# One core, hybrid decoder trunk: weight additions also given out during rotations, and another order of the last tokens' chain

## The chip, the core and the metric

The kernel runs on one core of a Trainium2 chip. A core has a matrix engine (TensorE, PE in the profile), whose weight loads are shown apart (PEld), and VectorE (DVE), ScalarE (ACT), GpSimd (POOL) and SyncE (SP). Each engine works through its own row of instructions in order and waits on semaphores for what others make. DMAs are given out by an engine (here nearly all by SP, some by POOL and ACT) and run beside it. The metric is the device time of one execution in microseconds (us); lower is better.

## The reference

The computation is one decoder layer in fp32 on 512 tokens of width 1024: a norm, an input projection, two token mixers (causal pooling, and a sparse attention with compressed, selected and window branches), a merge by sigmoid gates, `w_out`, a second norm, and an MLP of width 4096 with a squared ReLU, and a last norm. Cut to what matters here:

```python
def reference(x, norm_mix, w_in, ..., w_out, norm_mlp, w_ff1, w_ff2, norm_final):
    for l in range(DEPTH):
        h = rms_norm(x, norm_mix[l])
        proj = h @ w_in[l]
        u, q, kc, vc, ksl, vsl, kwn, vwn, g_nsa, g_merge = jnp.split(proj, IN_SPLITS, axis=-1)
        y_pool = pool_mixer(u, w_pool[l], pool_scale[l])
        y_nsa = nsa_mixer(q, kc, vc, ksl, vsl, kwn, vwn, g_nsa, ...)
        g_a, g_b = jnp.split(jax.nn.sigmoid(g_merge), 2, axis=-1)
        merged = g_a * (y_pool @ w_proj_pool[l]) + g_b * (y_nsa @ w_proj_nsa[l])
        x = x + merged @ w_out[l]
        h = rms_norm(x, norm_mlp[l])
        x = x + jnp.square(jax.nn.relu(h @ w_ff1[l])) @ w_ff2[l]
    return rms_norm(x, norm_final)
```

In the attention each of 16 heads has scores of queries against keys, a softmax under a causal mask, and a product with the values. The sequence is 512 long and the window 512, so that the work per head is a triangle of blocks of 128 x 128 to 128 x 512.

## The kernel before

**Number format.** A product in fp32 is made of three products of a faster type: each operand is split into a high part (ACT, names ending in H or h, L395 and L521) and a low part (DVE, names ending in L or l, L401 and L524), and high x high, low x high and high x low are summed in PSUM.

**Fewer products.** The large matrix products (the gates, `w_out`, `w_ff1`, `w_ff2`) are done by Strassen's scheme in Winograd's form: of four quarters of each operand seven products are made instead of eight. Their names stand in the code as `A11`, `A12`, `A22`, `S1` to `S4`. For these, sums of quarters of the weights are needed. The kernel forms these sums in HBM, ahead of their use: `make_sum` (L333 to L342) gives out a copy on SP (L340, tiles named S) behind a load of raw weights, and `add_sum` (L344 to L348) gives out a DMA on POOL (L348) that adds another quarter to what the copy has written. A list `jobs` holds the sums in a fixed order, `begun` those whose copy is given out and whose addition is not; the additions are taken from its front. Some sums are sums of earlier ones: job 93 copies job 91's sum (S_110_93 <- S_110_91) and adds to it. The finished sums are loaded on SP (L299) like other weights.

**The attention** takes from 172 to 365 us. It runs as 96 slots, eight pairs of heads by 12 slots. A slot has scores on PE (L1378), a masked maximum on DVE (L1400), exponentials on ACT (L1410), reciprocals on DVE (L1420), the weights on POOL (L1423: the P of a slot, times the reciprocal and the gate; one or two instructions of 128 x 128 to 128 x 512), and four slots later (LAG) the transposes of P on PE (L1440), their copies by ACT and DVE (L1451, L1456), and products with the values (L1474). Between these PE does products of the projections as filler (L565). Beside the slots run side steps: the rotation of the next head pair's queries (a DMA on SP, multiplications on POOL at L899) and the compressed branch's gates (POOL L1331 to L1335). `scored["rope"]` is true while a rotation is under way. In the slot loop an addition is given out behind the weights of the slot before, in every third slot in which no rotation is under way and more than two sums are begun:

```python
            if i > 7 and i % 3 == 0 and not scored["rope"] and len(begun) > 2:
                add_sum(last)
```

**The junction** lies between 430 and 460 us, where `w_out` ends and `w_ff1` begins. Class `Mixed` ends `w_out`: its last product S4 (L565) is added to x by `end` (L1821 to L1825) for the tokens 2 and 3 (a token here is a row block of 128 tokens), the others by `take` (L1827 to L1848). Then `scaled` norms a block into a tile xs (DVE L1612) and `to_fm` turns it (PE L1864, against `ident`), copies and splits it (ACT L1868, DVE L1871), and forms the sums T1 to T3 of the blocks (L1878, L1883). The first products of `w_ff1` are made by class `Group` (PE L635; its banks are emptied by ACT L650 and DVE L656 to L670): four key names in the order A11100, A11101, A12100, A12101, then the S1 ones, which need T1. The order in which PE takes the transposes and products comes from a scheduler that goes by readiness and priority in program order; `behind(x)` (L783) keeps an instruction behind x. After the junction the rest of `w_ff1` and `w_ff2` (class `Wide`, PE L1685, its results added to x at L1706) run without a break to 741 us, then the last norm.

Of the kernel before, what the change touches and what calls it, by code (L numbers as in the profile page):

```python
# [16 lines left out]
ALU = mybir.AluOpType  # L17
# [45 lines left out]
def trunk(ctx: ExitStack, tc: tile.TileContext, A, out):  # L63
# [548 lines left out]
    def until(ready):  # L612
        while not ready():
            assert side
            step_side()

    class Group:


# [6 lines left out]
        def pe(self, o):  # L626
            until(lambda: o not in self.NEEDS or self.NEEDS[o] in self.done)
            if not self.done:
                side.append(self.main())
            name, x, *at = self.X[o]  # L630
            until(lambda: self.of(x))
            moving = self.of(x)

            def mm(out, w, f, k, u, v, **kw):
                PE.matmul(out, w[u][:, k, 128 * f:128 * f + 128], moving[v][:, k, :], **kw)  # L635
            if not at:
                self.ps[name] = self.bank()
            product(self.ps[name], o + self.key, not at, mm)
            if at:
                side.append(self.last(name, *at))  # L640
            self.done.add(o)
# [30 lines left out]

    hT = (R1, R2)
    f_banks = [2]
    last_mm = [None]

    def fm_products(wH, wL, xT, sub=0, nk=8, tok=slice(0, S)):
        prods = []
# [104 lines left out]
    def behind(made):  # L783
        return tc.issue_after(made.ins)
# [463 lines left out]
    with ExitStack() as c2:  # L1248
# [249 lines left out]
        for i in range(n + LAG + PLAG):  # L1498
# [18 lines left out]
            if 0 <= i - 1 < n:  # L1517
                last = weight(i - 1)
                slot.update(long=i > 3 and slots[i - 1][1] == 1, scaled=last)
            if i > 7 and i % 3 == 0 and not scored["rope"] and len(begun) > 2:  # L1520
                add_sum(last)
            if 0 <= t < n:
                slot["low"] = turn_lo(t)
# [196 lines left out]
    with ExitStack() as c3:  # L1720
# [80 lines left out]
        class Mixed(Wide):  # L1801
# [18 lines left out]
            def end(self, f, ps):  # L1820
                yield  # L1821
                x = XX[:, 2 + f, 0:512]
                DVE.tensor_tensor(x, x, ps, op=ALU.add)
                square_sum(2 + f, 0, 1)
                yield from to_fm(2 + f)  # L1825

            def take(self, o, ps):  # L1827
                yield from super().take(o, ps)
# [12 lines left out]
                elif o == "A22":  # L1841
                    for t in range(2):
                        square_sum(t, 1)
                    xs = [scaled(t) for t in range(2)]
                    while "S1" not in self.done:
                        yield
                    for t in range(2):
                        yield from to_fm(t, xs[t])  # L1848

        def scaled(t):  # L1850
            xs = q3.tile([128, D], F32, tag="xs", bufs=2, name="xs")
# [3 lines left out]
        def to_fm(t, xs=None):  # L1855
# [5 lines left out]
            for a in range(2):  # L1861
                pt = bank()
                for k in range(4):
                    PE.transpose(pt[:, 128 * k:128 * k + 128], xs[:, 512 * a + 128 * k:512 * a + 128 * k + 128], ident)  # L1864
                src = pt[:, :].rearrange("p (k c) -> p k c", k=4)
                b = f"{a + 1}{th + 1}"
                if b != "12":
# [252 lines left out]
```

## Time and profile before

| | us |
|---|---|
| median of 3 runs | 768.44 (767.5 to 770.75) |
| the profiled execution | 766.66 |
| its span | 764.9 |
| attention | 172 to 365 |
| junction of w_out and w_ff1 | 430 to 452 |
| w_ff1 and w_ff2 | 452 to 741 |

The span is the time from the first to the last instruction in the trace; the profiled execution's time has a little around it. Its mean granted clock was 0.997 of full speed. PE is busy most of the span, so the page is read from the rows in which PE waits, and from the work around them; an idle DVE, ACT or POOL counts only where PE waits for what it makes.

### The profile page before, as it was taken

What the parts mean: (1) busy time and instruction counts of PE and PEld (TensorE: products, weight loads), DVE (VectorE), ACT (ScalarE), POOL (GpSimd) and SP (SyncE); (2) the same over time, 40 slices, a digit from 0 to 9 for tenths busy, and PEclk for the clock granted to TensorE, in tenths of its full rate; (3) what the DMA queues carried; (4) which work ended last, traced back from release to release, by engine and by line L of the source; (5) the groups of instructions that cost most, each with busy time, mean ns of one, the idle gap of its engine ahead of it and who ended that gap; (6) DMA issues with size and microseconds to landing.
All of it is one profiled execution on the core that took longest, in us unless ns stands there. A gap on an engine that the chain in (4) does not pass through costs nothing.

```text
span 764.9 us, 13254 instructions
## 1 busy us (share of the span) xinstructions
PE 752.9 (98%) x4661; PEld 669.7 (88%) x4661; DVE 670.8 (88%) x1282; ACT 513.2 (67%) x977; POOL 190.5 (25%) x269
## 2 busy tenths in 40 slices
PE   8999999999999999999999999999999999999996
PEld 7889999888888888888888799989998999899985
DVE  7998989549989889989689999998899788978897
ACT  7777655328878888898746576944774477447754
POOL 5001010117747876875000020111111111110001
PEclk9999999999999999999999999999999999999998
DMA  9869886986063945675383699979999999798532
GB/s 303 227 177 275 230 245 143 250 215 165 18 204 83 224 94 115 121 139 111 89 296 133 218 272 249 298 210 325 290 269 211 315 307 263 206 313 252 195 109 110
DMA packets 120285, 158.09 MB, mean 207 GB/s; under 512 B 6006, under 2 KB 88474, under 8 KB 119963
## 3 DMA queue, kind: packets, MB, share of 16 engines
q1 hardware_dynamic: 98058, 127.62, 51.2%
q0 software_dynamic: 21872, 28.84, 24.4%
q10 hardware_dynamic: 288, 0.79, 0.3%
q8 instruction: 37, 0.61, 0.3%
q14 instruction: 30, 0.24, 0.1%
HBM read 152.50 MB, written 59.77 MB: 278 GB/s over the span
## 4 chain that ended last, share of the span: by engine, by line
PE 87%; DVE 6%; ACT 2%; DMA 2%; issue 1%; POOL 1%; ACTq 0%; DVEq 0%; POOLq 0%; SPq 0%
PE psB L1685 21%; PE psB L635 21%; PE psF L565 18%; PE psV L635 5%; PE psB L565 4%; PE psS L1378 4%; PE psO L1474 3%; PE psT L1440 3%; PE psV L565 2%; PE psF L697 2%; DMA S<-w_ff 1%; PE psC L997 1%; DVE P L1400 1%; DVE PT L1456 1%; PE psT L565 1%
## 5 line engine op out<-in xcount | busy, mean ns | idle before, releaser
L348 POOL DMA_DIRECT2D S<-w_ff x44 | 49.3, 1124 | 334.1 <-DMA S<-w_ff 247.9
L395 ACT ACTIVATE wh<-raw 128x1024 fp32r<-128x1024 f32 x72 | 76.1, 1058 | 75.6 <-PE psB L635 28.3
L565 PE MATMUL psF<-R,wh 128*128 128x512 f32 x384 | 124.5, 400 | 0.0
L1423 POOL TENSOR_SCALAR P<-P,sm,GT 128x128 f32<-128x128 f32 (+3 forms) x128 | 91.0, 798 | 45.5 <-DVE sm L1420 25.4
L401 DVE TENSOR_TENSOR wl<-raw,wh 128x1024 fp32r<-128x1024 f32 x72 | 87.9, 1221 | 10.2 <-ACT wh L395 9.7
L565 PEld LDWEIGHTS psF<-R,wh 128*128 128x128 f32 x384 | 68.8, 188 | 11.2
L1410 ACT ACTIVATE P<-P,sm 128x128 f32<-128x128 f32 (+3 forms) x128 | 71.0, 557 | 9.6 <-DVE sm L1400 6.3
L565 PE MATMUL psF<-R,wl 128*128 128x512 f32 x192 | 75.5, 393 | 0.0
L521 ACT ACTIVATE wh<-raw 128x512 fp32r<-128x512 f32 (+1 forms) x76 | 45.1, 616 | 31.0 <-PE psF L565 21.2
L1400 DVE CUSTOM_DVE_ANT_0 P<-psS,cst 128x128 f32<-128x128 f32 (+3 forms) x128 | 59.5, 483 | 5.2 <-PE psT L1440 3.7
L395 ACT ACTIVATE w3h<-raw 128x1024 fp32r<-128x1024 f32 x36 | 38.1, 1058 | 36.9 <-PE psB L635 15.4
L524 DVE TENSOR_TENSOR wl<-raw,wh 128x512 fp32r<-128x512 f32 (+1 forms) x74 | 50.9, 697 | 11.0 <-ACT wh L521 10.2
L1451 ACT ACTIVATE PT<-psT 128x512 fp32r<-128x512 f32 (+2 forms) x96 | 49.0, 520 | 13.8 <-PE psT L1440 12.8
L1456 DVE TENSOR_TENSOR PT<-psT,PT 128x512 fp32r<-128x512 f32 (+2 forms) x96 | 56.2, 592 | 1.2 <-ACT PT L1451 1.0
L1440 PE MATMUL psT<-ident,P 128*128 128x128 f32 x320 | 50.2, 273 | 0.3 <-POOL P L1423 0.3
L401 DVE TENSOR_TENSOR w3l<-raw,w3h 128x1024 fp32r<-128x1024 f32 x36 | 44.0, 1222 | 5.6 <-ACT w3h L395 5.4
L1474 PE MATMUL psO<-PT,VV 128*128 128x256 f32 x320 | 48.5, 286 | 0.0
L635 PE MATMUL psB<-R,wh 128*128 128x256 f32 x336 | 46.7, 279 | 0.7 <-ACT GB L650 0.7
L1440 PEld LDWEIGHTS psT<-ident,P 128*128 128x128 f32 x320 | 39.5, 140 | 8.8 <-POOL P L1423 0.8
L635 PEld LDWEIGHTS psB<-R,wh 128*128 128x128 f32 x336 | 42.6, 188 | 1.1 <-ACT GB L650 0.9
L1474 PEld LDWEIGHTS psO<-PT,VV 128*128 128x128 f32 x320 | 42.2, 188 | 1.3 <-ACT PT L1451 0.3
L565 PEld LDWEIGHTS psF<-R,wl 128*128 128x128 f32 x192 | 36.0, 188 | 7.5
(450 smaller groups left out, 2074.6 us busy)
## 6 DMA issues: line engine op xcount, KB each, us to landing
raw<-w_ff SPq DMA_DIRECT2D x54, 512.0 KB, 6.0
S<-w_ff POOLq DMA_DIRECT2D x44, 512.0 KB, 8.5
raw<-S SPq DMA_DIRECT2D x44, 512.0 KB, 5.6
S<-w_ff SPq DMA_DIRECT2D x32, 512.0 KB, 7.6
raw<-w_in SPq DMA_DIRECT2D x31, 512.0 KB, 5.4
S<-S SPq DMA_DIRECT2D x12, 512.0 KB, 5.8
S_o<-w_out POOLq DMA_DIRECT2D x8, 512.0 KB, 7.8
raw<-w_proj_nsa SPq DMA_DIRECT2D x8, 512.0 KB, 4.5
```

The source lines that it names most:

```text
L395: ACT.activation(h, t, AF.Copy)
L401: DVE.tensor_tensor(l, t, h.bitcast(F32), op=ALU.subtract)
L524: eng.tensor_tensor(l[:, sl], t[:, sl], h[:, sl].bitcast(F32), op=ALU.subtract)
L565: PE.matmul(ps, a, b, start=first and j == 0, stop=last and j == n - 1, skip_group_check=True)
L635: PE.matmul(out, w[u][:, k, 128 * f:128 * f + 128], moving[v][:, k, :], **kw)
L1400: DVE.tensor_tensor_reduce(out=P[:, o:o + n].rearrange("p (a c) -> p a c", c=128), in0=s, in1=m, scale=1.0, scalar=3e38, op0=ALU.add, op1= ...
L1410: last_exp[:] = [ACT.activation(c, c, AF.Exp, bias=sm[:, 0, e:e + 1], scale=-1.0, accum_out=sm[:, 1, e:e + 1])]
L1423: r = POOL.tensor_scalar(P[:, o:o + n], P[:, o:o + n], sm[:, 2, e:e + 1], GT[:, qb, c + e:c + e + 1], op0=ALU.mult, op1=ALU.mult)
L1440: PE.transpose(pt[:, 128 * j:128 * j + 128], P[:, 128 * j:128 * j + 128], ident)
L1456: return DVE.tensor_tensor(dL, src, dH.bitcast(F32), op=ALU.subtract)
L1474: PE.matmul(ps[:, qb % 2, :, :], VV[:, k, b, g, :], t[:, j, :, :], start=False, stop=last and j == len(kbs) - 1 and t is tL, skip_group_ch ...
L1685: PE.matmul(ps[f], self.Y.of(y)[u][:, 2 * g + k, 128 * f:128 * f + 128], w[v][:, k, :], start=first and g == k == u == v == 0, stop=g == k ...
```

## The change

The sums are the same, and so are the instructions; what changes is when additions are given out, and the order at the junction. Four edits:

1. In the slot loop an addition is given out also while a rotation is under way, then in every sixth slot instead of every third.
2. In `Mixed.end` the addition of S4 to x, the sum of squares and `scaled` have a higher priority (60), and `to_fm` begins only after 30 (block 2) or 42 (block 3) products of the A11 group's keys with "10" have been given out (`fed`).
3. In `Mixed.take` only block 0 is normed ahead of S1; block 1 is normed behind the first addition of S1 to x.
4. The transposes of blocks 2 and 3 stand behind the last A11 product given out so far (`last_mm`), and the first A12100 product behind the last A11 product. `last_mm` is now made ahead of class `Group`.

```diff
--- before.py
+++ after.py
@@ -614,6 +614,8 @@
             assert side
             step_side()
 
+    last_mm, fed = [None], [0]
+
     class Group:
 
 
@@ -632,7 +634,12 @@
             moving = self.of(x)
 
             def mm(out, w, f, k, u, v, **kw):
-                PE.matmul(out, w[u][:, k, 128 * f:128 * f + 128], moving[v][:, k, :], **kw)
+                late = o + self.key == "A12100" and f == k == u == v == 0
+                with behind(last_mm[0]) if late else nullcontext():
+                    r = PE.matmul(out, w[u][:, k, 128 * f:128 * f + 128], moving[v][:, k, :], **kw)
+                if o == "A11":
+                    last_mm[0] = r
+                    fed[0] += self.key[:2] == "10"
             if not at:
                 self.ps[name] = self.bank()
             product(self.ps[name], o + self.key, not at, mm)
@@ -672,7 +679,6 @@
 
     hT = (R1, R2)
     f_banks = [2]
-    last_mm = [None]
 
     def fm_products(wH, wL, xT, sub=0, nk=8, tok=slice(0, S)):
         prods = []
@@ -1517,7 +1523,7 @@
             if 0 <= i - 1 < n:
                 last = weight(i - 1)
                 slot.update(long=i > 3 and slots[i - 1][1] == 1, scaled=last)
-            if i > 7 and i % 3 == 0 and not scored["rope"] and len(begun) > 2:
+            if i > 7 and i % (6 if scored["rope"] else 3) == 0 and len(begun) > 2:
                 add_sum(last)
             if 0 <= t < n:
                 slot["low"] = turn_lo(t)
@@ -1820,9 +1826,13 @@
             def end(self, f, ps):
                 yield
                 x = XX[:, 2 + f, 0:512]
-                DVE.tensor_tensor(x, x, ps, op=ALU.add)
-                square_sum(2 + f, 0, 1)
-                yield from to_fm(2 + f)
+                with tc.high_priority(60):
+                    DVE.tensor_tensor(x, x, ps, op=ALU.add)
+                    square_sum(2 + f, 0, 1)
+                    xs = scaled(2 + f)
+                while fed[0] < (30, 42)[f]:
+                    yield
+                yield from to_fm(2 + f, xs)
 
             def take(self, o, ps):
                 yield from super().take(o, ps)
@@ -1841,11 +1851,13 @@
                 elif o == "A22":
                     for t in range(2):
                         square_sum(t, 1)
-                    xs = [scaled(t) for t in range(2)]
+                    xs = scaled(0)
                     while "S1" not in self.done:
                         yield
-                    for t in range(2):
-                        yield from to_fm(t, xs[t])
+                    with behind(summed[0]):
+                        other = scaled(1)
+                    yield from to_fm(0, xs)
+                    yield from to_fm(1, other)
 
         def scaled(t):
             xs = q3.tile([128, D], F32, tag="xs", bufs=2, name="xs")
@@ -1861,7 +1873,8 @@
             for a in range(2):
                 pt = bank()
                 for k in range(4):
-                    PE.transpose(pt[:, 128 * k:128 * k + 128], xs[:, 512 * a + 128 * k:512 * a + 128 * k + 128], ident)
+                    with behind(last_mm[0]) if th else nullcontext():
+                        PE.transpose(pt[:, 128 * k:128 * k + 128], xs[:, 512 * a + 128 * k:512 * a + 128 * k + 128], ident)
                 src = pt[:, :].rearrange("p (k c) -> p k c", k=4)
                 b = f"{a + 1}{th + 1}"
                 if b != "12":
```

What this does to the rows of the engines is shown at four places, before and after. Lines below the first edit are 4, 6 or 13 higher in the changed kernel (L1423 is L1429, L899 is L905, L635 is L639, L1706 is L1712, L1864 is L1877, L1823 is L1830); L348 and L401 are the same.

POOL, at the head pair that is under way at 302 us; first before. P is the slot's weights, S a weight sum, rx and rs the rotation, cw and PC the compressed branch.

```order
L1423 TENSOR_SCALAR P<-P,sm,GT 128x384
L348 DMA S_111_95<-w_ff 512x1x256
L1423 TENSOR_SCALAR P<-P,sm,GT 128x384
L899 TENSOR_TENSOR rx<-rx,cst 128x256
L1331 TENSOR_TENSOR c_3794<-c_3794,GT 128x8
L1332 TENSOR_TENSOR cw<-cw,c_3794 128x8x32
L1423 TENSOR_SCALAR P<-P,sm,GT 128x512
L899 TENSOR_TENSOR rs<-rs,cst 128x256
L1334 TENSOR_SCALAR PC<-cw 128x4x64
L1335 TENSOR_TENSOR PC<-cw,PC 128x4x64
L1423 TENSOR_SCALAR P<-P,sm,GT 128x512
```

Then the changed kernel.

```order
L1429 TENSOR_SCALAR P<-P,sm,GT 128x384
L348 DMA S_111_95<-w_ff 512x1x256
L1429 TENSOR_SCALAR P<-P,sm,GT 128x384
L348 DMA S_100_83<-w_ff 512x1x256
L905 TENSOR_TENSOR rx<-rx,cst 128x256
L1429 TENSOR_SCALAR P<-P,sm,GT 128x512
L905 TENSOR_TENSOR rs<-rs,cst 128x256
L1337 TENSOR_TENSOR c_3797<-c_3797,GT 128x8
L1338 TENSOR_TENSOR cw<-cw,c_3797 128x8x32
L1340 TENSOR_SCALAR PC<-cw 128x4x64
L1341 TENSOR_TENSOR PC<-cw,PC 128x4x64
L1429 TENSOR_SCALAR P<-P,sm,GT 128x512
```

A second addition (S_100_83) now stands one weight behind the first, ahead of the rotation, and the compressed branch's steps have moved behind a 128x512 weight.

POOL at the last head pair, from 331.6 us in the trace of before.

```order
L1423 TENSOR_SCALAR P<-P,sm,GT 128x384
L348 DMA S_200_88<-w_ff 256x1x512
L1423 TENSOR_SCALAR P<-P,sm,GT 128x384
L1423 TENSOR_SCALAR P<-P,sm,GT 128x512 x2
L348 DMA S_100_83<-w_ff 512x1x256
L1423 TENSOR_SCALAR P<-P,sm,GT 128x128 x4
L1423 TENSOR_SCALAR P<-P,sm,GT 128x256 x2
L348 DMA S_201_89<-w_ff 256x1x512
```

The same place in the changed kernel.

```order
L1429 TENSOR_SCALAR P<-P,sm,GT 128x384
L348 DMA S_110_91<-w_ff 512x1x256
L1429 TENSOR_SCALAR P<-P,sm,GT 128x384
L1429 TENSOR_SCALAR P<-P,sm,GT 128x512 x2
L348 DMA S_110_92<-w_ff 512x1x256
L1429 TENSOR_SCALAR P<-P,sm,GT 128x128 x2
L348 DMA S_110_93<-w_ff 512x1x256
L1429 TENSOR_SCALAR P<-P,sm,GT 128x128 x2
L1429 TENSOR_SCALAR P<-P,sm,GT 128x256 x4
```

The additions here are now those of the sums 91, 92 and 93, and the last one stands between the first and the second two of the four 128x128 weights; before, those four stood together and an addition came behind the next two.

DVE at the junction, from the first normed blocks on (xs), before.

```order
L1612 SCALAR_TENSOR_TENSOR xs<-x_4903,sq,gB_4914 128x512 x2
L1602 RECIPROCAL sq<-sq 128x1
L1612 SCALAR_TENSOR_TENSOR xs<-x_4903,sq,gB_4914 128x512 x2
L1706 TENSOR_TENSOR x_4903<-x_4903,psB 128x512 x2
L401 TENSOR_TENSOR W1L<-raw_5221,W1H 128x1024
L1595 TENSOR_SCALAR sq<-sq 128x1
L401 TENSOR_TENSOR wl_5170<-raw_5239,wh_5169 128x1024
L1595 TENSOR_SCALAR sq<-sq 128x1
L1871 TENSOR_TENSOR R_65<-psB,R_64 128x4x128 x2
L401 TENSOR_TENSOR w3l<-raw_5257,w3h 128x1024
L1871 TENSOR_TENSOR R_65<-psB,R_64 128x4x128 x2
L1823 TENSOR_TENSOR x_4903<-x_4903,psB 128x512 x2
```

And in the changed kernel.

```order
L1618 SCALAR_TENSOR_TENSOR xs<-x_4903,sq,gB_4914 128x512 x2
L1712 TENSOR_TENSOR x_4903<-x_4903,psB 128x512 x2
L1608 RECIPROCAL sq<-sq 128x1
L401 TENSOR_TENSOR W1L<-raw_5221,W1H 128x1024
L1601 TENSOR_SCALAR sq<-sq 128x1
L1618 SCALAR_TENSOR_TENSOR xs<-x_4903,sq,gB_4914 128x512
L1601 TENSOR_SCALAR sq<-sq 128x1
L1618 SCALAR_TENSOR_TENSOR xs<-x_4903,sq,gB_4914 128x512
L1884 TENSOR_TENSOR R_65<-psB,R_64 128x4x128
L1830 TENSOR_TENSOR x_4903<-x_4903,psB 128x512
L1884 TENSOR_TENSOR R_65<-psB,R_64 128x4x128 x2
L401 TENSOR_TENSOR wl_5170<-raw_5239,wh_5169 128x1024
```

The two additions of S1 to x (L1706, now L1712) stand ahead of the second pair of xs, and S4's addition to the first of the later blocks (L1823, now L1830) ahead of two of the splits.

PE at the junction, around the first A12100 products (R_64 or R_65 against wh_5169) and the later blocks' transposes (ident,xs), before.

```order
L635 MATMUL psB<-R_64,W1L 128x256 x4
L635 MATMUL psB<-R_64,wh_5169 128x256
L635 MATMUL psB<-R_65,wh_5169 128x256
L1864 MATMUL psB<-ident,xs 128x128 x4
L635 MATMUL psB<-R_64,wh_5169 128x256
L635 MATMUL psB<-R_65,wh_5169 128x256
L1864 MATMUL psB<-ident,xs 128x128 x4
L635 MATMUL psB<-R_64,W1H 128x256
```

And in the changed kernel.

```order
L639 MATMUL psB<-R_65,W1H 128x256
L1877 MATMUL psB<-ident,xs 128x128 x4
L639 MATMUL psB<-R_64,W1H 128x256
L639 MATMUL psB<-R_65,W1H 128x256
L639 MATMUL psB<-R_64,W1L 128x256 x4
L1877 MATMUL psB<-ident,xs 128x128 x4
L639 MATMUL psB<-R_64,wh_5169 128x256
L639 MATMUL psB<-R_65,wh_5169 128x256
```

The first A12100 products stood between A11's, with transposes among them; now they stand behind all of A11's products and behind the transposes. Further ahead, of the nine transposes that stood ahead of S4's first product four are left there, and the others follow between the products. On SP two pairs of rows trade places: the copy of sum 86 stands behind that of sum 91, and the copy of sum 93 behind the load of one more raw weight tile.

## The prediction

> **What bounds the kernel now.** I read the page's head and the shares of its chain first, then the busy time by stage.
>
> ```profile
> span 764.9 us, 13254 instructions
> PE 752.9 (98%) x4661; PEld 669.7 (88%) x4661; DVE 670.8 (88%) x1282; ACT 513.2 (67%) x977; POOL 190.5 (25%) x269
> PE 87%; DVE 6%; ACT 2%; DMA 2%; issue 1%; POOL 1%; ACTq 0%; DVEq 0%; POOLq 0%; SPq 0%
> 140.00:172.00 32.00, 32.00 (x147) 26.63 (x146) 14.92 (x26) 8.29 (x14) 5.16 (x7) 1.00 0.83 220
> 172.00:365.00 193.00, 191.35 (x1239) 168.45 (x1238) 173.84 (x579) 164.93 (x447) 130.45 (x193) 1.00 0.57 126
> 430.00:452.00 22.00, 20.70 (x123) 17.82 (x122) 21.33 (x36) 16.28 (x36) 5.36 (x5) 1.00 0.93 278
> 452.00:741.00 289.00, 289.00 (x1911) 265.45 (x1911) 261.21 (x313) 182.28 (x244) 26.42 (x24) 1.00 0.92 258
> ```
>
> The window rows give start:end, length, busy time (and count) of PE, PEld, DVE, ACT and POOL, the granted clock, the DMA share and GB/s. PE is busy 98% of the span. In the attention (172 to 365) it is idle 193.00 - 191.35 = 1.65 us, at the junction between w_out and w_ff1 (430 to 452) 1.30 us, and from 452 to 741 never. So taking work off another engine is worth nothing in itself; the change can win only what PE waits for, and can lose wherever it gives PE a new wait. The list of waits (engine, tile, line, what it waited for: us in all, times, longest) says what there is to win:
>
> ```profile
> PE psB L635 <- ACT GB L650: 0.7, 1, 0.7
> PE psB L565 <- DVE x L1706: 0.6, 1, 0.6
> PE psT L1440 <- POOL P L1423: 0.3, 1, 0.3
> ```
>
> **The junction** (edits 2, 3 and 4). The timeline's rows give start, duration, engine, line, operation and count, and in brackets the idle time ahead and what ended it.
>
> ```profile
> 437.04 1.14 PE L1864 MATMUL psB<-ident,xs 128*128 128x128 f32 x9
> 438.80 0.47 PE L565 MATMUL psB<-W1H,mH 128*128 128x512 f32 x1 [0.61 <-DVE x L1706]
> 436.64 1.42 DVE L1612 SCALAR_TENSOR_TENSOR xs<-x,sq,gB 128x512 f32<-128x512 f32 x2
> 437.97 1.28 DVE L1706 TENSOR_TENSOR x<-x,psB 128x512 f32<-128x512 f32 x2
> 448.21 0.60 ACT L650 ACTIVATE GB<-psB 128x512 f32<-128x512 f32 x1 [0.35 <-PE psB L635]
> 448.86 0.51 PE L635 MATMUL psB<-R,wh 128*128 128x256 f32 x2 [0.69 <-ACT GB L650]
> 459.15 0.52 PE L635 MATMUL psB<-R,wh 128*128 128x256 f32 x3
> 455.37 0.69 DVE L1883 TENSOR_TENSOR R<-GB,R 128x512 fp32r<-128x512 f32 x1
> ```
>
> Before, DVE writes the second token's two xs halves (1.42 us) and only then adds S1 to x, which empties the bank that S4's first product needs: PE does nine transposes and stands 0.61. In the change's order the two additions stand ahead of that pair, and four transposes ahead of S4's first product. The first addition can then run at about 436.8 and end 0.6 later, and four transposes from 437.04 at 1.14 / 9 each end at about 437.55: PE enters S4 with no wait, and the other transposes follow between S4's products. The work is the same, so the gain is the wait: **-0.6**.
>
> The second wait is 0.69 ahead of A12100's first product (the row at 448.86): A12100 stood among A11101's products and its bank came free when ACT had copied GB (0.60 from 448.21). In the change all 30 products of the A11 groups that were left stand ahead of A12100, with the transposes of the last two tokens between them, so that the copy lies beside PE work: **-0.7**. A small rest (my step by step sum of both orders gives 1.6, not 1.3) I take as **-0.1**; together **-1.4**, with -1.0 and -1.6 as ends.
>
> What is late next? The new order puts the last token's transposes later on PE, and behind them lie the copy, the low part and T1's sums, which the S1100 products need. Before, T1's low part ends at 455.37 + 0.69 = 456.06 and the products start at 459.15: 3.1 us of room. They would now start at about 457.7. The high priority around `end` moves S4's addition and the xs ahead of weight splits, so T1's low part stays at about 456: 1.6 us of room, no new wait. The weight splits that give way (L401) are wanted only by products behind those of S4.
>
> **Additions in rotation slots** (edit 1). The order shows the same number of POOL DMAs and of everything else; three additions that stood ahead of the attention go into its slots, and the others come earlier there. PE is busy 32.00 of 32.00 us from 140 to 172, so those three give nothing back. In the slots an addition holds POOL for 0.76 us (from its start at 270.87 to the next weight's at 271.63, below) and for whatever it waits; behind it on POOL stand the weights, and PE's transposes four slots later wait for these. Most new places have room:
>
> ```profile
> 203.68 0.77 POOL L1423 TENSOR_SCALAR P<-P,sm,GT 128x512 f32<-128x512 f32 x1
> 206.20 0.60 PE L1440 MATMUL psT<-ident,P 128*128 128x128 f32 x4
> ```
>
> The weight ends at 204.45, its transposes come at 206.20: 1.75 of room for 0.76. So the additions now given at about 194, 203, 218, 233, 245, 265, 279, 291 and 325 cost **0**; a queue that ran late twice in a row would take the cover away, at 0.3 to 0.5 each. On SP two copies trade places with a neighbour; a load there is given out microseconds ahead of its use, so **0** again. Three places are different.
>
> *The wait of POOL at 266* goes. POOL stood for the copy of S_92's sum:
>
> ```profile
> 260.24 10.00 DMA S<-w_ff
> 270.87 1.19 POOL L348 DMA_DIRECT2D S<-w_ff  x1 [4.98 <-DVE PT L1456]
> 271.63 3.85 POOL L1423 TENSOR_SCALAR P<-P,sm,GT 128x128 f32<-128x128 f32 x5
> 275.53 0.63 PE L1440 MATMUL psT<-ident,P 128*128 128x128 f32 x4 [0.32 <-POOL P L1423]
> ```
>
> The copy (a row of the chain) landed at 270.24 and POOL went on at 270.87. The releaser named, DVE, had long been done: the copy ended last. In the change this addition comes at 336, and POOL's weights here run 5 us earlier: **-0.4** (0.32 in the row, up to 0.5).
>
> *Two additions nearly side by side at 303.* S_83's addition now stands one weight behind S_95's, ahead of a rotation and the head's compress steps:
>
> ```profile
> 302.00:309.20 7.20, 7.20 (x47) 6.40 (x46) 7.12 (x21) 7.02 (x16) 7.04 (x10) 1.00 0.68 116
> 308.48 0.78 POOL L1423 TENSOR_SCALAR P<-P,sm,GT 128x512 f32<-128x512 f32 x1
> 309.48 0.60 PE L1440 MATMUL psT<-ident,P 128*128 128x128 f32 x4
> ```
>
> POOL is busy 7.04 of 7.20 us (the window's row) up to the weight's end at 309.26, and the transposes start at 309.48: 0.22 of room, and at most 0.16 of idle time, for 0.76. That is 0.4 to 0.5, and with the semaphore's way **+0.6**; the ends are 0 (the compress steps, 2.5 us, slip behind the weight as they did in neighbouring slots) and +1.2 (PE's next slot loses as much again).
>
> *The last pair* carries the sum. The change puts S_93's addition between the first and the second two of its four 128x128 weights. It needs the copy S_93 <- S_91, and that copy reads what S_91's addition, now at about 332.2, writes.
>
> ```profile
> 265.01 0.89 POOL L1423 TENSOR_SCALAR P<-P,sm,GT 128x128 f32<-128x128 f32 x2
> 332.22 1.06 POOL L348 DMA_DIRECT2D S<-w_ff  x1
> 335.56 1.18 POOL L348 DMA_DIRECT2D S<-w_ff  x1
> 336.26 2.64 POOL L1423 TENSOR_SCALAR P<-P,sm,GT 128x128 f32<-128x128 f32 x4
> DMA to landing us min/median/max: 6.1/6.3/6.6
> DMA to landing us min/median/max: 4.7/5.2/10.2
> 343.70 0.38 PE L1440 MATMUL psT<-ident,P 128*128 128x128 f32 x2
> ```
>
> The landing rows are those of POOL's additions (L348) from 310 to 350 and of SP's copies (L340) from 200 to 345. S_91's addition lands at 332.2 + 6.1 to 6.6 = 338.3 to 338.8, and SP gives out the copy right then; it lands 4.7 to 5.2 later, at 343.0 to 344.0. POOL, which would reach the addition at about 337.6, stands until then. It goes on 0.63 after a landing (270.24 to 270.87), its next weight starts 0.76 later (270.87 to 271.63), and two 128x128 weights take 0.89 (the row at 265.01; by 2.64 / 4 each it would be 1.3): with 343.4 as the landing, 345.7. PE wants them at 343.70, and before had almost 5 us of room (336.26 + 2.64 = 338.9). So **+2.2**, with 1.6 and 3.5 as ends; below them lies 0, if the landings are shorter than any in these rows. Behind on POOL stand the last 128x256 weights; their transposes are queued behind the late ones on PE, so they are not late a second time.
>
> Sum: -1.4 - 0.4 + 0.6 + 2.2 = **+1.0**. The profiled execution took 766.66 (span 764.9), so 767.7; the median of the runs shown, 768.44, stands 1.8 above it: **769.4**.
>
> **The rivals.** All times are medians on that scale.
>
> *No wait at the last pair* (0.18). S_91's addition and its copy together would have to need under about 9 us. Speaking against: the shortest landings of the rows make 6.1 + 4.7 = 10.8. For: the order of the other transfers differs then. Price: the 2.2 goes, -1.2, **767.2**. The Trainium skill's page "DMA: Bandwidth & Descriptors", section "Anatomy of one DMA — SWDGE (gpsimd) path", gives a transfer of this kind about 2.0 us plus its bytes over 436 GB/s; for 512 KB that is an estimate of 3.2 us, two in a row 6.4, and POOL would not wait at all. The trace's rows, 6.1 at least, disagree, so by that rule alone the case gets 1 in 20.
>
> *The clock falls at the last pair* (0.17, the slower end). The tail shows what an idle PE does:
>
> ```profile
> 757.58 0.39 PE L565 MATMUL psB<-R,y22L 128*128 128x512 f32 x1
> 760.00:761.00 1.00, 0.00 (x0) 0.00 (x0) 0.33 (x1) 0.36 (x1) 0.00 (x0) 0.80 0.70 274
> 763.00:764.80 1.80, 0.00 (x0) 0.00 (x0) 0.00 (x0) 0.00 (x0) 0.00 (x0) 0.50 0.03 9
> ```
>
> The last matmul ends at 757.97. In the slice from 760 the mean clock is 0.80, which is 0.50 from about 760.6 on, 2.6 us after the end of work; it stays at 0.50 to the end. A wait of 2.6 us or more at 343.70 would thus halve the clock, which decides once the copy lands after about 344.0. Four us at half clock lose 2.1: 3.2 + 2.1 for 2.2 gives +4.1 in all, **772.5**. With the longest landing of the copies, 10.2, POOL would come at about 351.3: +7.6 and the clock, about 778; this I give 0.03 of the 0.17. The Trainium skill ("TensorE: Matmul & The Clock Gate", section "Part 1: The HAM clock gate") has the clock halve after an idle window of about 3.4 us that runs freely, and that much busy time release it; by that a wait of 2.6 would fall into it only by its phase.
>
> *The junction's gain is given back* (0.12), the case in which that edit doesn't do what it says. After 452 PE never waits, but one product starts just as its operand is ready:
>
> ```profile
> 522.32 1.22 DVE L401 TENSOR_TENSOR w3l<-raw,w3h 128x1024 fp32r<-128x1024 f32 x1
> 523.59 0.50 PE L1685 MATMUL psB<-w3l,y22H 128*128 128x512 f32 x1
> 483.60 1.23 DVE L401 TENSOR_TENSOR wl<-raw,wh 128x1024 fp32r<-128x1024 f32 x1 [0.56 <-ACT wh L395]
> ```
>
> DVE ends w3l at 523.54 and PE takes it at 523.59; DVE has no idle time between 483.60 and there. PE can be earlier at 523 only if DVE is, and DVE can gain only in idle time up to 483.6, such as the last row's 0.56. It waited there for ACT, which works behind PE and should move up with it; that speaks against. If they don't, the 1.4 is lost: +2.4, **770.9**.
>
> **How the numbers follow.** The forecast has 0.48, the rivals 0.18, 0.17 and 0.12, anything else 0.05. Predicted: 769.4. Low end: no wait at the last pair with the junction at -1.6 and no loss at 309 gives 766.66 - 2.0 + 1.8 = 766.4, and the runs shown lie down to 0.9 below their median, so 766.0. High end: the clock's case, 772.5, with 0.3 for it: 772.8. Within 0.5% (3.8 us, about what a measurement of this kernel tells from no change) lie 764.6 to 772.3: the forecast, the first and the third rival and a part of the clock's case, 0.83. Slower: most of the clock's case, 0.12. Faster: 0.05, for a wait that no row names.
>
> **What would show it.** Right: no wait of PE on x or GB between 430 and 452, S1100 about 1.4 earlier against the junction's start; no wait of POOL of 5 us near 266; POOL idle for 5 us or more ahead of an addition between two pairs of 128x128 weights, and PE waiting for P of the weights line about 344 for 1.6 to 3.5 us; a wait of about 0.5 near 309. Wrong: S_93's copy landed when POOL asks; a granted clock under 1.00 there; a new wait on w3l or wl between 452 and 741; SP late with a raw load in the attention; any of the nine early additions showing up as a PE wait.

## The result and the profile after

The changed kernel took 772.07 us (median of 7 runs, 771.09 to 773.41) against 768.44 for the kernel before (7 runs in all, with the same median as the 3 shown ahead): a ratio of 1.0053, 95% interval 1.0041 to 1.0064. That is 2.7 us above the predicted 769.4 and inside the range given. The profiled execution took 772.07 as well, 5.4 us more than the one of before.

The page's head and the windows of the changed kernel (the same columns as before; the attention now runs to about 371, the junction from 436 to 458):

```profile
span 770.3 us, 13248 instructions
PE 755.2 (98%) x4661; PEld 671.2 (87%) x4661; DVE 673.5 (87%) x1282; ACT 513.2 (67%) x977; POOL 190.6 (25%) x269
172.00:371.00 199.00, 192.92 (x1233) 168.98 (x1233) 176.67 (x579) 164.51 (x445) 133.74 (x195) 0.99 0.61 128
436.00:458.00 22.00, 22.00 (x133) 19.14 (x132) 21.02 (x35) 16.77 (x38) 5.35 (x5) 1.00 0.86 263
```

PE's idle time at the junction went from 1.30 us to none; in the attention it went from 1.65 to 6.08, over a stretch that is 6 us longer. The page's sums of busy time tell nothing of this: PE is at 98% in both, and ACT and POOL did the same work in the same time. Only DVE has 2.7 us more, with the same instructions. From the list of waits, longest first, the rows of the attention that matter here:

```profile
PE psT L1446 <- POOL P L1429: 2.1, 1, 2.1
PE psS L1384 <- DVE sm L1406: 1.6, 2, 1.3
PE psT L1354 <- DVE PT L1462: 1.1, 1, 1.1
PE psT L1446 <- DVE sm L1426: 0.4, 1, 0.4
```

The first is the forecast's wait at the last pair. The second and third, near 207 and 291 us, stood in no forecast; the fourth is at the place near 309, but PE waits there for DVE, and not for POOL as forecast.

**The last pair** came as worked out, with a fall of the clock behind it. Timeline rows of the changed kernel, PE's, POOL's and SP's, then windows with the clock in the third column from the end:

```profile
335.10 1.18 POOL L348 DMA_DIRECT2D S<-w_ff  x1
341.37 0.49 SPq L340 DMA_DIRECT2D S<-S  x1
347.10 1.18 POOL L348 DMA_DIRECT2D S<-w_ff  x1 [6.04 <-DVE R L1289]
346.34 0.40 PE L1384 MATMUL psS<-KL,Q 128*128 128x512 f32 x1
348.82 0.89 PE L1446 MATMUL psT<-ident,P 128*128 128x128 f32 x2 [2.08 <-POOL P L1429]
349.00:350.00 1.00, 0.91 (x4) 0.67 (x4) 0.00 (x0) 0.26 (x1) 1.00 (x4) 0.57 0.98 56
351.00:352.00 1.00, 1.00 (x3) 0.79 (x3) 1.00 (x5) 0.72 (x2) 1.00 (x3) 0.50 1.26 203
352.00:353.00 1.00, 1.00 (x7) 0.93 (x6) 1.00 (x3) 0.69 (x2) 1.00 (x2) 0.72 0.64 99
```

S_91's addition is given out at 335.10, the copy that reads it at 341.37, and POOL stands 6.04 us until the copy has landed; PE stands 2.08. The releaser in POOL's row, DVE, is misnamed again. PE's last matmul ended at 346.74; the slice from 349 has a mean clock of 0.57, so it halved (1.00 to 0.50) at about 349.1, 2.4 us later, when PE had already been back for 0.3 us. The slice from 352 gives its return at about 352.5. So 3.4 us ran at half speed, about 1.7 us lost. The Trainium skill ("TensorE: Matmul & The Clock Gate", section "Part 1: The HAM clock gate") has about 3.4 us of busy time release the clock; this stretch agrees. The idle window of about 3.4 us that the Trainium skill states in the same section for the fall does not agree: PE had been idle for 2.08 us.

**Near 207** the new wait begins on DVE. Rows of before, and of the changed kernel:

```profile
206.00 0.79 DVE L524 TENSOR_TENSOR wl<-raw,wh 128x512 fp32r<-128x512 f32 x1
206.22 1.18 POOL L899 TENSOR_TENSOR rs<-rs,cst 128x256 f32<-128x256 f32 x1
```

```profile
203.28 1.07 POOL L348 DMA_DIRECT2D S_o<-w_out  x1
206.14 1.16 POOL L1429 TENSOR_SCALAR P<-P,sm,GT 128x512 f32<-128x512 f32 x1
206.36 2.19 DVE L524 TENSOR_TENSOR wl<-raw,wh 128x512 fp32r<-128x512 f32 x1
206.88 1.11 POOL L905 TENSOR_TENSOR rs<-rs,cst 128x256 f32<-128x256 f32 x1
209.15 0.39 PE L1384 MATMUL psS<-KH,Q 128*128 128x256 f32 x1 [1.30 <-DVE sm L1406]
```

The same low-part split of a weight (L524) took 0.79 us before and 2.19 after. Before, it came when POOL was about to be free and POOL's rotation waited for it (1.18 for a step that takes 0.74 elsewhere). After the addition at 203.28 POOL was late and had its weights and the rotation back to back; the split ended 0.56 behind the rotation's end (207.99 and 208.55). Behind it on DVE stood the minimum of the scores, and PE waited for that.

**Near 291 and 309** DVE's steps are stretched in the same way. First the rows of before, then those of the changed kernel:

```profile
283.07 0.41 DVE L892 TENSOR_TENSOR rx<-rx,rs 128x256 f32<-128x256 f32 x1
288.41 0.69 DVE L936 TENSOR_TENSOR Q<-rx,Q 64x512 fp32r<-64x512 f32 x1
304.73 0.79 DVE L524 TENSOR_TENSOR wl<-raw,wh 128x512 fp32r<-128x512 f32 x1
```

```profile
283.91 1.10 DVE L898 TENSOR_TENSOR rx<-rx,rs 128x256 f32<-128x256 f32 x1
290.06 1.15 DVE L942 TENSOR_TENSOR Q<-rx,Q 64x512 fp32r<-64x512 f32 x1
293.24 0.51 PE L1354 MATMUL psT<-identR,PC 128*128 128x128 f32 x4 [1.09 <-DVE PT L1462]
306.84 1.45 DVE L524 TENSOR_TENSOR wl<-raw,wh 128x512 fp32r<-128x512 f32 x1
310.05 0.63 PE L1446 MATMUL psT<-ident,P 128*128 128x128 f32 x4 [0.41 <-DVE sm L1426]
311.47 0.78 POOL L1429 TENSOR_SCALAR P<-P,sm,GT 128x512 f32<-128x512 f32 x1
312.31 0.66 PE L1446 MATMUL psT<-ident,P 128*128 128x128 f32 x4
```

At 291 it is not a split of weights but the rotation's addition (0.41 before, 1.10 after) and the low part of Q (0.69 and 1.15), 1.2 us together. At 309 it is a split, 0.7 longer. The weight whose lateness the forecast priced ends at 312.25 here, and its transposes start at 312.31 with no wait in their row; PE's wait stands one group of transposes earlier, at 310.05.

### The profile page after: what moved, and what is told of

It is laid out like the page before. It is cut to its first block, busy times and chain, and to the rows that moved or that the text cites. A ratio compares the mean times of both kernels' runs of the same rounds, so it can differ in the third digit from the quotient of the medians.

```text
span 770.3 us, 13248 instructions
## 1 busy us (share of the span) xinstructions
PE 755.2 (98%) x4661; PEld 671.2 (87%) x4661; DVE 673.5 (87%) x1282; ACT 513.2 (67%) x977; POOL 190.6 (25%) x269
## 4 chain that ended last, share of the span: by engine, by line
PE 89%; DVE 6%; ACT 2%; issue 1%; DMA 1%; POOL 0%; SPq 0%; DVEq 0%; ACTq 0%; POOLq 0%
PE psB L1691 22%; PE psB L639 20%; PE psF L565 19%; PE psV L639 5%; PE psB L565 4%; PE psO L1480 4%; PE psT L1446 4%; PE psS L1384 4%; PE psV L565 2%; PE psF L703 2%; DVE P L1406 1%; PE psC L1003 1%; DVE PT L1462 1%; ACT P L1416 1%; DMA raw<-w_in 1%
## 5 line engine op out<-in xcount | busy, mean ns | idle before, releaser
L348 POOL DMA_DIRECT2D S<-w_ff x44 | 50.3, 1147 | 312.6 <-DMA S<-w_ff 241.6
L1429 POOL TENSOR_SCALAR P<-P,sm,GT 128x128 f32<-128x128 f32 (+3 forms) x128 | 92.7, 824 | 53.4 <-DVE sm L1426 25.9
L401 DVE TENSOR_TENSOR wl<-raw,wh 128x1024 fp32r<-128x1024 f32 x72 | 87.6, 1219 | 10.3 <-ACT wh L395 9.7
L524 DVE TENSOR_TENSOR wl<-raw,wh 128x512 fp32r<-128x512 f32 (+1 forms) x74 | 52.7, 723 | 10.6 <-ACT wh L521 10.1
L401 DVE TENSOR_TENSOR w3l<-raw,w3h 128x1024 fp32r<-128x1024 f32 x36 | 43.9, 1220 | 5.7 <-ACT w3h L395 5.4
L639 PE MATMUL psB<-R,wh 128*128 128x256 f32 x336 | 46.3, 279 | 0.0
L639 PEld LDWEIGHTS psB<-R,wh 128*128 128x128 f32 x336 | 42.5, 188 | 0.2
```

Source lines behind the costliest of these rows:

```text
L401: DVE.tensor_tensor(l, t, h.bitcast(F32), op=ALU.subtract)
L524: eng.tensor_tensor(l[:, sl], t[:, sl], h[:, sl].bitcast(F32), op=ALU.subtract)
L639: r = PE.matmul(out, w[u][:, k, 128 * f:128 * f + 128], moving[v][:, k, :], **kw)
L1429: r = POOL.tensor_scalar(P[:, o:o + n], P[:, o:o + n], sm[:, 2, e:e + 1], GT[:, qb, c + e:c + e + 1], op0=ALU.mult, op1=ALU.mult)
```

## The experiments

To place the time, I give each run's PE stalls in its profiled execution: the time between the starts of neighbouring matmuls, less the median for the first one's form, in us. A dash is a place with none over 0.15. "All" is the sum of the stalls over 0.15 from 20 us on; the sum hangs on that limit, so only its differences are read.

```
                  207   291   309   last pair       275   junction   all
before             -     -     -     -              0.5   1.6         4.1
changed           1.5   1.3   0.6   2.3 + clock     0.3    -          9.1
e1_junction        -     -     -     -              2.5    -          4.4
e2_slots          1.5   1.3   0.6   1.6 + 0.3       0.3   1.4         9.2
e3_hold93         1.5   1.3   0.7    -              0.3    -          5.4
e4_idle           0.2   0.4   0.4    -              0.2    -          3.2
e4b_idle2          -    0.9   0.9    -              0.4    -          4.7
e5_copy           1.1   0.5   0.4    -              0.5    -          4.3
e8_hold92          -     -    0.4    -              0.3    -          3.4
e7_skip3           -     -    0.4    -              0.3    -          2.8
e9_odd             -    1.3    -     -              0.5    -          5.6
```

Theory at the start: the junction gains 1.5 us; the loss is the slot edit's, by POOL's time at four places. Rivals: the junction's gain is given back; PE is late at the last pair anyway; the transfers do the damage, not POOL's time.

**The two parts apart.** `e1_junction` puts the slot loop's old condition back into the changed kernel:

```diff
-            if i > 7 and i % (6 if scored["rope"] else 3) == 0 and len(begun) > 2:
+            if i > 7 and i % 3 == 0 and not scored["rope"] and len(begun) > 2:
```

> Only edits 2 to 4 (the junction), the slot loop as before. Theory: the junction alone gains what PE waited for there, about 1.5 us (2.00 us of stalls between 430 and 450 in the trace of before, 0.47 in that of the change), and nothing gives it back: 766.9 against 768.4 for before, 1.4 to 1.6 us earlier at every landmark behind 460 us, no wait of 5 us less on POOL at 266 (it stays). Rival, the gain is given back at w3l near 523: 768.4, and a new PE wait there.

Measured: 765.93 against 766.71, ratio 0.9987 (0.9978 to 0.9996). The junction's window has PE busy throughout, as in the changed kernel:

```profile
430.00:452.00 22.00, 22.00 (x129) 18.98 (x128) 20.13 (x34) 16.58 (x37) 5.35 (x5) 1.00 0.85 263
277.37 0.64 PE L1446 MATMUL psT<-ident,P 128*128 128x128 f32 x4 [2.36 <-DVE PT L1462]
271.08 1.19 POOL L348 DMA_DIRECT2D S<-w_ff  x1 [5.30 <-DVE sm L1426]
273.55 3.01 DVE L524 TENSOR_TENSOR wl<-raw,wh 128x512 fp32r<-128x512 f32 x1
272.77 3.24 POOL L1429 TENSOR_SCALAR P<-P,sm,GT 128x128 f32<-128x128 f32 x6
275.96 1.17 POOL L905 TENSOR_TENSOR rx<-rx,cst 128x256 f32<-128x256 f32 x1
```

The gain at the junction is there and nothing gives it back behind 452, but of the forecast's 1.4 the medians show 0.8 (0.3 to 1.7). The wait near 275, 0.3 in the execution of before, is 2.36 in this one, and the rows show the same cause as near 207: POOL stood 5.30 for S_92's copy, then ran its late weights back to back from 271.8 to 276.0, and a split that came at 273.55 got through at 276.55, after the last of them. In the trace of before POOL was as late, and the split lost only 0.5. So the price of POOL's wait at that place was not the same in these two executions; whether it differs between executions of one kernel is not shown.

`e2_slots` is the kernel before with the first edit alone.

> Only edit 1 (additions during rotations), the junction as before. Theory: the slot edit costs all of the loss, some 5 to 7 us of one execution (waits of 1.3 near 207 on DVE, 1.1 near 291 on DVE, 0.6 near 309 on POOL, 2.1 near 346 on POOL and up to 2 us at half clock behind that, less 1 us of small waits that go): 773.5 against 768.4. Rival, the losses come from the two parts together (an addition's place moved by the junction's scheduling): below 770, with one of the four waits missing.

Measured: 772.5 against 766.71, ratio 1.0074 (1.0061 to 1.0087). All four waits are there and the junction's stand as before; the slot edit carries the whole loss. The rival falls. In this execution the clock stayed at 1.00 behind a last-pair stall of 1.6.

**The last pair.** `e3_hold93` puts S_93's addition behind the attention's last weights. `latest[0]` is the weights instruction given out last; the other rows of all engines stay as they are.

```diff
-        to, _, q = jobs[begun.popleft()]
+        n = begun.popleft()
+        to, _, q = jobs[n]
+        if n == 25:
+            behind = latest[0]
...
+                latest[0] = last
```

> The changed kernel with S_93's addition held behind the attention's last weights; every other row on every engine stays in its place. Theory: the wait for that addition's copy is all there is at the last pair: the wait of 2.1 us near 346 goes, and with it the fall of the clock behind it: 768.5 to 769.5 against 772.1 for the change, granted clock 1.00 in every slice from 340 to 360, the other waits (207, 291, 309) as they are. Rival, POOL or PE is late there anyway (the weights or the copies of P): a wait of 1 us or more stays near 344 to 346, and the time is above 770.5.

Measured: 767.85 against 766.71, ratio 1.0015 (1.0007 to 1.0024), where the changed kernel has 1.0053: 0.38%, 2.9 us, for one addition's place, each ratio against its own runs of before. That is below the time expected. PE is busy throughout there, at full clock:

```profile
345.00:350.00 5.00, 5.00 (x34) 4.41 (x33) 4.86 (x18) 4.98 (x16) 3.58 (x5) 1.00 0.36 100
```

The other three waits stand. The rival falls: nothing else was late at the last pair.

**POOL's time, or the transfer?** `e4_idle` is the junction's edits with a multiplication of a spare tile on POOL in the three slots whose additions stand ahead of the waits at 207, 291 and 309; `e4b_idle2` has two of them.

```diff
+            if i in (18, 54, 66):
+                with tc.issue_after(last.ins):
+                    POOL.tensor_tensor(idle, idle, idle, op=ALU.mult)
             if i > 7 and i % 3 == 0 and not scored["rope"] and len(begun) > 2:
```

> Edits 2 to 4, the slot loop's condition as before, and in slots 18, 54 and 66 (where the change has the additions ahead of the waits near 207, 291 and 309) a multiplication of a spare 128x224 tile on POOL, about 0.7 us, with no DMA. Theory: what costs is POOL's time; the weights behind it slip by 0.7 and then run at the same time as DVE's work, which is stretched by it: waits near 207 (1 to 1.5 us), 291 (about 1) and 309 (about 0.5) come back without any DMA, 769 to 770. Rival, the additions' transfers or their issue through memory do the damage: no such waits, the time of the junction's edits alone, 766.9.

Measured: 766.49 against 766.71, ratio 0.9995 (0.9984 to 1.0007). The multiplication took 0.57, and brought back 0.2, 0.4 and 0.4, and 0.6 of the time against `e1_junction`, far from the 769 to 770 expected. The theory's size failed.

> The kernel of the idle multiplications with two of them instead of one in slots 18, 54 and 66, 1.05 to 1.15 us of POOL per slot, which is what the record of an addition's issue shows (1.07 to 1.18). Theory: an addition costs POOL its whole record, not the 0.7 from its start to the next start; twice the idle work then brings the waits back that one of 0.57 did not: about 1.3 near 207, about 1 near 291, 1 near 309, and the low-part split near 206 stretched beyond 1.5 us: 768.5 to 769.5. Rival, the waits are the DMA's own doing (its transfer or its issue): at 207 and 291 no more than with one, below 767.5.

Measured: 766.68 against 767.24, ratio 0.9996 (0.9978 to 1.0014), below the 768.5 to 769.5 expected. At 291 and 309 stalls of 0.9 came back with no DMA at all, and with them the rotation's addition on DVE at 282.49 took 1.15 and the split at 305.06 took 1.29; at 207 none did, and a new one of 0.9 stood near 237. The rows near 207 show why more idle work cost less there:

```profile
206.02 0.71 DVE L524 TENSOR_TENSOR wl<-raw,wh 128x512 fp32r<-128x512 f32 x1
206.17 1.21 POOL L1431 TENSOR_SCALAR P<-P,sm,GT 128x512 f32<-128x512 f32 x1
```

POOL's steps now fell so that the split came first and POOL's weights waited for it, 1.21 for 0.77. So the length of POOL's delay alone does not decide at this place; these rows suggest that it is who holds when the other comes.

`e5_copy` has a plain copy of 512 KB given out by POOL in the same slots, in 16 rows, to a tile that nobody reads.

```diff
+            if i in (18, 54, 66):
+                with tc.issue_after(last.ins):
+                    POOL.dma_start(spare_sum, jobs[0][0])
```

> Edits 2 to 4, and in slots 18, 54 and 66 a plain copy of 512 KB from HBM to HBM given out by POOL, in 16 long rows instead of 512 short ones, to a tile that nobody reads. If POOL's time for an issue goes by its rows: the issue is short (below 0.5 us) and the waits at 207 and 291 stay away although the same bytes move (below 767.5). If the transfer does the damage, or if any issue costs POOL over 1 us: the waits come back, 768.5 to 769.5; the issue's own record tells these two apart.

Measured: 767.06 against 767.24, ratio 0.9995 (0.9983 to 1.0007). The rows near 207:

```profile
203.46 0.72 POOL L1529 DMA_DIRECT2D spare<-S_g  x1
206.38 0.76 POOL L1430 TENSOR_SCALAR P<-P,sm,GT 128x512 f32<-128x512 f32 x1
206.53 1.87 DVE L524 TENSOR_TENSOR wl<-raw,wh 128x512 fp32r<-128x512 f32 x1
207.12 0.73 POOL L905 TENSOR_TENSOR rs<-rs,cst 128x256 f32<-128x256 f32 x1
```

The issue took 0.72, less than an addition's 1.07, and the split was held for 1.87 by POOL's weights and rotation. The wait at 207 came back (1.1), that at 291 in part (0.5). The median shows little of it. So neither the additions' rows nor their adding is needed; that a transfer's memory traffic has no part in it is not shown by this run. The stall of 291 in `e4b_idle2` had no transfer; at 207 no run brought the wait back without one.

**The collision by itself.** `e6_port` leaves the layer out and only does groups of eight splits on DVE, alone and beside POOL's two forms. The groups ran into each other, so that some POOL steps fell into other groups than meant; the rows, of one execution, show single meetings all the same.

> Not the layer: it only does groups of eight low-part splits on DVE (128x512, one of the trunk's forms) alone, beside POOL's weights form (128x512), beside POOL's rotation form (128x256), beside two additions' issues, beside both POOL forms in turn without and with an issue ahead, and groups that read PSUM. Theory: DVE and POOL hinder each other where both read and write SBUF: a split takes about 0.7 alone and well over 1 us beside back-to-back POOL work, POOL's weights take longer than 0.78 as well; from PSUM the hindrance is smaller. Rival, they don't and the stretched split near 206 waited for something else: 0.7 in every group.

```profile
7.58 1.88 DVE L91 TENSOR_TENSOR low<-x 128x512 fp32r<-128x512 f32 x3
13.95 7.00 POOL L97 TENSOR_SCALAR P<-P,sm 128x512 f32<-128x512 f32 x1
61.08 3.43 DVE L91 TENSOR_TENSOR low<-x 128x512 fp32r<-128x512 f32 x3
61.80 2.16 POOL L97 TENSOR_SCALAR P<-P,sm 128x512 f32<-128x512 f32 x1
21.92 0.77 POOL L97 TENSOR_SCALAR P<-P,sm 128x512 f32<-128x512 f32 x1
21.43 1.27 DVE L94 TENSOR_TENSOR low<-psT,x 128x512 fp32r<-128x512 f32 x2
34.58 17.49 DVE L91 TENSOR_TENSOR low<-x 128x512 fp32r<-128x512 f32 x1
```

Three splits alone take 1.88 (0.60 from start to start). One POOL weights step that came while DVE had splits back to back took 7.00 instead of 0.77: it got in when the run of splits ended. From 58.7 on they took turns, and three splits took 3.43. But ahead of that one split (the row at 34.58) took 17.49, beside POOL's weights and rotation in turn without a gap; so taking turns is not the rule when both have work. Splits that read one operand from PSUM (L94) and POOL's weights ran side by side at full speed. The theory of hindrance holds. The Trainium skill ("SBUF — State Buffer", section "SBUF: two separate sides") calls the pair of SBUF ports that DVE and GpSimd share an exclusive lock that an instruction keeps for its whole length, and names DVE's instructions with two SBUF inputs among those concerned; these rows agree. They go further in one point: the other side can stay out for a run of instructions, 7.00 and 17.49 here and 3.01 near 275 above.

**What is left when the collisions go.** `e8_hold92` is the junction's edits with S_92's addition held behind the weights given out last when the program asks for it, as S_93's above (`n == 22`).

> Edits 2 to 4 alone, with S_92's addition held behind the weights that were given out when the program asked for it, in the last pair; nothing else moves. Theory: POOL's wait for that copy near 270, which made PE wait 0.3 us in one execution of before and 2.4 in that of the junction's edits alone, goes with it: no wait near 275, 764 to 765.5 against 766.7 for before. Rival, POOL is late at the last pair instead, where it now gives out three additions within three weights: a wait of 0.5 to 1.5 near 345, no gain against the junction's edits alone.

Measured: 765.56 against 767.24, ratio 0.9977 (0.9963 to 0.9991), the lowest of the ratios. No stall over 0.3 near 275, none at the last pair; the rival falls. Against `e1_junction` (0.9987, another session) the gain is not clear of the scatter.

`e7_skip3` is the changed kernel with both additions held and none in three slots:

```diff
-            if i > 7 and i % (6 if scored["rope"] else 3) == 0 and len(begun) > 2:
+            if i > 7 and i % (6 if scored["rope"] else 3) == 0 and len(begun) > 2 and i not in (18, 54, 66):
...
+        if n in (22, 25):
+            behind = latest[0]
```

> The changed kernel without additions in slots 18, 54 and 66, and with S_92's and S_93's additions held behind weights as in the two runs above. Theory: the slots' loss is these three places and the last pair, and nothing else: no PE wait of 0.5 or more near 207, 291, 309 and 346, the additions that stay in rotation slots cost nothing, 764.5 to 766, 0.2 to 0.4% below before and level with the junction's edits with S_92 held. Rival, additions in rotations cost wherever they stand: waits of 0.5 or more at the slots that now have them (near 204, 214, 217, 266), above 767.

Measured: 765.65 against 766.83, ratio 0.9984 (0.9975 to 0.9993). Neither 207 nor 291 nor the last pair has a stall; one of 0.4 stays near 307, behind an addition at 300.95 that has its like in the kernel before (301.53). The additions that stay in rotation slots, and the three moved in from ahead of the attention, cost nothing that shows.

`e9_odd` has S_93 held and the rotation's additions in slots 15, 21, 27 and so on (`i % 6 == 3`).

> The changed kernel with S_93's addition held, and the rotation's additions in the sixth slots between (15, 21, 27 and so on) instead of 12, 18, 24. Theory: a place costs only where POOL's slip makes its work meet a low-part split of DVE or eats the last of POOL's room; other places have other meetings, so the waits near 207 and 291 of the change go and the time falls from 767.9 (with S_93 held) to 765.5 to 767. Rival, it is the number of additions during rotations: three waits of 0.5 to 1.5 at other places, 767.5 to 769.

Measured: 769.23 against 766.83, ratio 1.0032 (1.0021 to 1.0044), above what the theory expected. The wait at 207 went, that at 291 stayed (the addition now at 285.10 stood ahead of it), and stalls of 0.2 to 0.5 came near 282 and 315. At 291 it is again the rotation's addition on DVE, 2.31 at 283.12. So place counts, but a shift to other slots did not find better ones, and that the number of additions has no part is not shown; half of the rival's account holds.

## Why the prediction was right or wrong

- **The junction, -1.4: right.** The stalls there fell from 1.6 to none over 0.15, and PE behind 452 had no new wait (`e1_junction`). The third rival falls. In medians `e1_junction` shows 0.8 of it.
- **The last pair, +2.2: right**, in mechanism and size: 2.08 of wait, by the addition, its copy, and the way back to the weights as worked out. `e3_hold93` took it away. The first rival, no wait, falls, and with it the estimate of 6.4 us for the two transfers: S_91's addition was given out at 335.10 and the copy that reads it at 341.37, 6.3 later, not 3.2, and from the one addition to the next it was 12.0 us. The estimate also used the figure for a GpSimd transfer for the copy, which SP gives out; and with 6.4 POOL, at the addition by 337.6, would still have waited about 1 us (332.2 + 6.4).
- **Near 309, +0.6: the number by luck.** The stall is 0.6, but by another way. The weight that was to be late was in time for its transposes (312.25 and 312.31); PE waited ahead of that, at 310.05, behind DVE, whose split took 1.45 for 0.79. In `e2_slots` and `e3_hold93` it is the same (1.48 and 1.58, stalls of 0.6 and 0.7).
- **POOL's wait at 266, -0.4: right in what goes, open in size.** 0.2 showed in the profile of the change; `e1_junction` shows that the same wait of POOL may cost PE 2.4.
- **The clock: half right, given 0.17.** In the profiled execution it fell, and cost about 1.7. The condition named, a wait of 2.6 or more, was not met: a wait of 2.08 was enough. In three of the seven runs of the change the mean granted clock is 0.995, and they took 772.07 to 772.48; in three it is 0.998 or 0.999 (771.09, 771.53 and 773.41); one has 0.997 (771.18), which the half clock behind the last matmul can give by itself, as in the execution of before. So it seems to fall in some executions and not in others. The kernel before is not free of it: in one session 3 of its 29 executions have 0.995 or 0.996 and took 769.9 to 772.0, none of them profiled. (By its own terms 4 us at half clock lose 2.0, not 2.1, and the case of the longest copy comes to about 777, not 778.)
- **The step that failed: "So the additions now given at about 194, 203, 218, ... cost 0".** It put beside the addition's time on POOL only the room between POOL's weights and PE's transposes. At 203 that room held: no transposes waited. What waited was DVE, and so PE, which the prediction had named as a sign that it is wrong (an early addition that shows up as a PE wait). DVE's split of weights reads and writes the same memory as POOL's steps; it lost 1.4 us there and PE 1.3. At 291 its rotation's addition and Q's low part lost 1.2, and PE 1.1. These two places are stalls of 2.7 us in the profile of the change. On the scale of the profiled execution the forecast was 767.7 and the time 772.07, 4.4 more: the 2.7 and the clock's 1.7. That the median lies only 2.7 above the forecast is luck in part: the forecast added 1.8 because the median of before stood that far above its profiled execution, and the change's median is its profiled execution; in the three later sessions the median of before was 766.71, 767.24 and 766.83. The time is inside the range because the high end made room for the clock with a wait of 3.2 us; no case had new waits of DVE. A second, smaller flaw was in the price: 0.76 from one start to the next was taken for the addition's time on POOL, where its record and the weights behind it show over 1 us.

Which of the two engines gets through when both wait is not settled. In the trace of before and in `e4_idle` a split got in between two POOL steps, in `e5_copy` and near 275 in `e1_junction` it did not, with gaps that look alike.

## What to carry to other kernels

Work that is put on an idle engine is to be checked against every engine that shares a resource with it, not only against those that wait for its results: a GpSimd that is 68% busy (130.45 of 193 us in the attention) was full at the places where VectorE had its SBUF to SBUF steps. An accumulating DMA that needs an earlier one's copy belongs where nothing stands behind it on its engine; a hold of one addition was worth 2.9 us, more than the whole junction. And the stall of 2.08 us on TensorE cost another 1.7 us through the clock.

## What was not expected of the hardware

- A VectorE split (128x512, two SBUF operands, 0.68 us alone) took 3.01 us in the layer, and 17.49 in the run without the layer, beside GpSimd steps that followed each other without a gap, and a GpSimd step (0.77 alone) took 7.00 us beside such splits; with one operand in PSUM neither lost anything.
- The clock halved 2.4 us after the end of the last matmul ahead of the wait, although matmuls had begun again 0.3 us earlier, and came back 3.4 us later.
- Near 275 the same rows in the same order cost PE 0.3 us in the execution of before and 2.4 in that of `e1_junction`, with POOL's late start there 0.2 us apart.
